# Two layers of a hybrid Fourier, Hyena and attention backbone: two pairs instead of three for the input projection's weights, staging slots for the last first modulation weights, one modulation group in the output projection

## The chip, the cores and the metric

The kernel runs on one core of one Trainium2 chip. The metric is the device time of one execution in microseconds (us); the median of three runs before the change is 2942.47, from 2940.16 to 2943.14. The engines are TensorE (PE in the profile, its weight loads PEld), VectorE (DVE), ScalarE (ACT), GpSimd (POOL) and SyncE (SP); DMAs are issued here by SyncE, GpSimd and ScalarE, each in the order of its own queue.

## What is computed

Two layers on 1024 latent tokens and 256 context tokens of width 1024. Layer 0 mixes with a Fourier transform on half of the channels and a Hyena operator (two long convolutions with generated filters) on the other half, with one input and one output projection; layer 1 is neighbourhood attention. Each layer ends in a modulated feed-forward. The reference, cut:

```python
def ada_mod(cond, w, b):                 # six groups: shift, scale, gate, twice
    m = (jax.nn.silu(cond) @ w + b)[..., None, :]
    return jnp.split(m, 6, axis=-1)

def hyena_filters(L, w1, b1, freq, w2, b2, w3):
    ...
    h = jnp.sin(freq * (z @ w1 + b1))
    h = jnp.sin(freq * (h @ w2 + b2))
    h = (h @ w3).reshape(L, 2, HY_ORDER, HY_CH)
    ...
    h = h / jnp.sum(jnp.abs(h), axis=(0, 1), keepdims=True)
    ...
def mixer_ab(u, w_in, w_out, conv_w, conv_b, w1, b1, freq, w2, b2, w3, skip):
    p = u @ w_in
    y_f = fourier_mix(p[..., :FOURIER_CH])
    y_h = hyena_mix(p[..., FOURIER_CH:], conv_w, conv_b, w1, b1, freq, w2, b2, w3, skip)
    return jnp.concatenate([y_f, y_h], axis=-1) @ w_out
...
    sh1, sc1, g1, sh2, sc2, g2 = ada_mod(c, ada_w[i], ada_b[i])
    u_lat = modulate(rms_norm(h_lat, norm1_g[i]), sh1, sc1)
    ...
    h_lat = h_lat + g1 * y_lat
    h_lat = h_lat + g2 * swiglu(modulate(rms_norm(h_lat, norm2_g[i]), sh2, sc2),
                                ffn_w_gate[i], ffn_w_up[i], ffn_w_down[i])
```

## The kernel before

**Products in pieces.** Activations and weights are split into a high and a low part (`split`, L345 to L352: ScalarE casts the high part at L349, VectorE subtracts for the low part at L351), and a product is three products of parts on TensorE (`mm`, L345). A weight block is loaded into a staging slot of tag `ws` (four slots of 128x1024), and its high and low parts go to `wh` and `wl` (two slots each).

**Pools.** `S4` gives one of 21 tiles of 128x1024, `S2` one of 35 of 128x512; results wait in eight PSUM banks (`ps`, `pq`).

**The order.** The code is a set of generators that are advanced in turn by hand. The instructions are then ordered for each engine by a scheduler that simulates a timeline from its own costs; so the order on an engine follows the code only in part, and tiles' slots are handed out in it. On an engine, and on each DMA queue, instructions run in that order. `ld` puts a load on SyncE's queue (L330), `ldr` on GpSimd's (L336).

**The start.** `ada_first` computes the modulation groups 1 and 0 (scale and shift of layer 0) on TensorE: sixteen tiles of `in_ada_k` (0.5 MB each, GpSimd's queue), each multiplied with the two condition columns into two banks; then `columns` turns the rows into columns (a copy to `g` at L509, eight 2x2 products). Beside it run the filter network (casts and subtractions for its last layer at L734 to L737) and the first norm (squares at L665 on ScalarE and L668 on VectorE).

**The input projection** (`in_proj`) has 16 blocks of 128 output channels. The first two run together, the rest one by one, each with 72 products of 256 or 512 columns. Its weights come by `weights3`, in which every third block's two parts take `ws` slots. Work of other generators is dealt between the eight steps of a block (`filled`) by tables of rates, one number for each block: `long` (the long filters: `filter_raw`, which multiplies the network's output with `in_w3` and a window, `filter_sum` and `spectrum_l`), `filt` (the filters for the context), and `ada`, the modulation groups 2 and 3, whose weights load into `ws` slots and which VectorE reduces (`ada_group`, L567, four instructions a step, eight steps a group).

**From there to the feed-forward.** After the projection the filters' spectra and the transforms of the data follow, then `inverse_last` (the last inverse transforms; L1211 and L1218 add and subtract spectra there, L1376 are its products and L1408 its copies). Group 4 of the modulation runs in the loop over `inverse_last`, with `ws` slots on SyncE's queue. `out_proj` (products L1716) fetches a weight block ahead and takes what is left of that generator. The feed-forward and layer 1 follow; in the second feed-forward the weights' parts alternate between `ws` and `wh`/`wl` slots by the counter `p3`, which `weights3` also advances.

Of the kernel before, what the change touches and what calls it, by code (L numbers as in the profile page):

```python
# [18 lines left out]
P = 128  # L19
# [239 lines left out]
class Builder:  # L259
# [119 lines left out]
    def weights3(self, src):  # L379

        self.p3 = (self.p3 + 1) % 3
        st = self.W("ws", "ws")
        tags = ("ws", "ws") if self.p3 == 0 else ("wh", "wl")
        hi, lo = self.pair2(tags)
        self.ld(st, src)
        self.split(st, hi, lo)
        return hi, lo

# [108 lines left out]
    def ada_first(self):  # L497
# [7 lines left out]
        def columns(m, ps):  # L505
            col = self.PS()
            for j in (0, 1):
                row = self.G()
                nc.vector.tensor_copy(row[0:2, :], ps[j][0:2, :])  # L509
                for k in range(4):  # L510
                    nb = 4 * j + k
                    self.mm(col[:, 2 * nb:2 * nb + 2], row[0:2, k * P:(k + 1) * P], self.ident[0:2, 0:2], True, True)
# [9 lines left out]
        for m in (1, 0):  # L522
            ps[m] = [self.PP(), self.PP()]
            for kb in range(KB):
                w = self.S4()
                self.ldr(w, a["ada_k"][m, kb])
                for j in (0, 1):
                    self.mm(ps[m][j][0:2, :], cond[:, 2 * kb:2 * kb + 2], w[:, j * 512:(j + 1) * 512], kb == 0, kb == KB - 1)
                yield
        columns(1, ps[1])  # L530
        columns(0, ps[0])
# [11 lines left out]
    def ada_group(self, l, m, conds, where):  # L543
# [12 lines left out]
        ready = [load(m * 8)] if where == "ws" else []  # L556
        for nb in range(m * 8, m * 8 + 8):
            if where != "ws" or nb < m * 8 + 7:
# [18 lines left out]
    def late_groups(self, ms):  # L577

        self.load_cond(wide=False)
        for m in ms:  # L580
            yield from self.ada_group(0, m, (0, 1), "ws")
# [166 lines left out]
    def filter_raw(self, sq, raws, os=(0, 1)):  # L748
# [4 lines left out]
        for o in os:  # L753
            for j in (0, 1):
                st[(o, j)] = self.S2()
                self.ld(st[(o, j)], a["w3"][:, (2 * j + o) * HC:(2 * j + o + 1) * HC])
        yield
        for o in os:
            for eo, op in ((0, ADD), (1, SUB)):
# [4 lines left out]
                w3[(o, eo)] = (hi, lo)  # L764
        yield
        for b in range(nb):
            for s, lh in ((0, self.ta[sq]), (1, self.tb[sq])):
                w = self.S2()
                self.ld(w, a["win_" + sq][b, s])
# [261 lines left out]
    def in_proj(self, u, norm, fill, four, conv):  # L1031
# [40 lines left out]
        pairs = [self.weights3(a["w_in"][nb]) for nb in (0, 1)]  # L1072
# [17 lines left out]
        for i, nb in enumerate(order[2:], 2):  # L1090
            wh, wl = self.weights3(a["w_in"][nb])
# [1368 lines left out]
    def run(self):  # L2460
# [28 lines left out]
        def filters():  # L2489
            for o in (0, 1):  # L2490
                tot = self.filter_sum("l", o, raws["l"][o])
                for k, _ in enumerate(self.filter_raw("l", raws["l"], (o,))):
                    if k > 2 and k % 2:
                        next(tot)
                    yield
                yield from self.spectrum_l(o, raws["l"][o], tot)

        long = filters()
        ada = self.late_groups((2, 3))
# [17 lines left out]
        self.in_proj(u, ng, ((long, (4,) * 8 + (6, 0)), (filt, (0,) * 9 + (3, 3, 3, 3, 2)), (ada, (0, 0, 0) + (1,) * 10 + (2,))), fc, cc)  # L2517
# [292 lines left out]
```

## Time and profile before

| | |
|---|---|
| median of three runs | 2942.47 us |
| profiled execution | 2941.1 us, its span 2939.3 |
| granted TensorE clock, mean | 0.974 |
| TensorE, 0 to 68 us (start) | 45.7 us busy |
| TensorE, 68 to 500 us (input projection, filters) | 392 us busy of 432 |
| TensorE, 500 to 590 us (transforms) | 89.0 us busy of 90 |
| TensorE, 590 to 725 us (inverse transforms) | 108.5 us busy of 135 |
| TensorE, 725 to 820 us (output projection) | 95.0 us busy of 95 |
| TensorE, 820 to 2939 us (feed-forward, layer 1) | 2074.7 us busy of 2119 |

The times of the profile count from the span's start. "Busy" includes time at half clock, where a product takes twice as long; the granted clock of a stretch says how much of that there was. In a row of the timeline stand start, duration, engine, line, operation, tiles and the count of instructions run together; in brackets stands the engine's idle time before it and what ended that.

### The profile page before, as it was taken

Reading aid. Unit: us, or ns where it says so; the run is one execution under the profiler, and the core shown is the slowest. Engines: PE = TensorE matmul, PEld = TensorE weight load, DVE = VectorE, ACT = ScalarE, POOL = GpSimd, SP = SyncE. Lnnn points to the kernel's source line nnn. Section 1 sums busy time; section 2 is a strip of 40 time slices with the busy share of each in tenths; the row PEclk is TensorE's granted clock in tenths of the full one; section 3 lists DMA queues with packets and bytes.
Section 4 is the critical chain, followed back from the end, with each engine's and each line's share of the span. In section 5 each row is a group of like instructions: output and inputs, shape, how many; then the busy total and the mean of one; then the engine's idle time right before and its main releaser. Section 6 shows DMA issues by size and latency. Waiting matters only on the chain. (4 is left out here: it accounts for less than half of the span.)

```text
span 2939.3 us, 43728 instructions
## 1 busy us (share of the span) xinstructions
PE 2804.8 (95%) x15570; PEld 2343.3 (80%) x15570; DVE 2078.2 (71%) x3657; ACT 1319.4 (45%) x2259; POOL 538.3 (18%) x867
## 2 busy tenths in 40 slices
PE   6989998978999999999999999999999999999998
PEld 2768776867899888888888988888887788888886
DVE  4677788767586888877777526777777987664555
ACT  2533324533355333333445426777765533333433
POOL 1120232350101121213020002333221022111000
PEclk8999898988999999999999999999999999999999
DMA  6244636674456565658895435678766276434763
GB/s 248 73 164 163 190 94 204 202 232 168 151 193 220 193 202 193 206 195 312 300 311 184 158 115 152 181 184 191 206 213 219 83 266 228 162 110 166 228 194 130
DMA packets 298217, 557.35 MB, mean 190 GB/s; under 512 B 82057, under 2 KB 128331, under 8 KB 297999
## 3 DMA queue, kind: packets, MB, share of 16 engines
q1 hardware_dynamic: 236046, 371.53, 40.8%
q0 software_dynamic: 59648, 178.83, 17.3%
q10 hardware_dynamic: 2304, 4.20, 0.4%
q8 instruction: 123, 2.02, 0.3%
q14 instruction: 96, 0.78, 0.1%
HBM read 407.10 MB, written 119.80 MB: 179 GB/s over the span
## 5 line engine op out<-in xcount | busy, mean ns | idle before, releaser
L1883 PE MATMUL ps<-s,s 128*128 128x512 f32 x1976 | 488.2, 389 | 2.5 <-DVE s L351 1.9
L1883 PEld LDWEIGHTS ps<-s,s 128*128 128x128 f32 x1976 | 370.6, 188 | 80.9 <-DVE s L351 2.6
L345 PE MATMUL ps<-s,wh 128*128 128x256 f32 (+1 forms) x1752 | 404.1, 333 | 8.3 <-DVE s L1026 5.1
L345 PEld LDWEIGHTS ps<-s,wh 128*128 128x128 f32 x1752 | 295.6, 192 | 42.1 <-ACT s L1024 5.3
L345 PE MATMUL pq<-s,wh 128*128 128x512 f32 (+1 forms) x872 | 267.2, 382 | 9.6 <-ACT wh L349 5.5
L345 PE MATMUL ps<-s,wl 128*128 128x256 f32 (+1 forms) x876 | 266.5, 330 | 1.6 <-DVE wl L351 1.5
L349 ACT CAST s<-s 128x1024 fp32r<-128x1024 f32 (+2 forms) x192 | 172.7, 927 | 201.6 <-DMA s<-d 166.2
L2056 PE MATMUL ps<-s,s 128*128 128x512 f32 (+1 forms) x1000 | 259.6, 383 | 3.1 <-DVE s L351 3.0
L351 DVE TENSOR_TENSOR wl<-ws,wh 128x1024 fp32r<-128x1024 f32 (+1 forms) x141 | 167.7, 1190 | 132.9 <-ACT wh L349 128.4
L345 PE MATMUL ps<-s,s 128*128 128x65 f16 (+5 forms) x2754 | 237.9, 239 | 20.1 <-DVE s L351 5.0
L349 ACT CAST wh<-ws 128x1024 fp32r<-128x1024 f32 (+1 forms) x141 | 144.6, 1025 | 231.5 <-PE ps L345 88.2
L349 ACT CAST s<-t 128x512 fp32r<-128x512 f32 (+2 forms) x238 | 133.9, 582 | 240.5 <-PE ps L1883 72.8
L351 DVE TENSOR_TENSOR s<-s,s 128x1024 fp32r<-128x1024 f32 (+2 forms) x170 | 190.8, 1154 | 53.2 <-ACT s L349 50.6
L2056 PEld LDWEIGHTS ps<-s,s 128*128 128x128 f32 x1000 | 184.5, 188 | 41.1 <-DVE s L351 4.8
L351 DVE TENSOR_TENSOR s<-t,s 128x512 fp32r<-128x512 f32 (+2 forms) x238 | 150.8, 649 | 77.5 <-ACT s L349 55.5
L1883 PE MATMUL ps<-s,wh 128*128 128x512 f32 x616 | 191.2, 390 | 0.0
L345 PEld LDWEIGHTS pq<-s,wh 128*128 128x128 f32 x872 | 159.1, 190 | 38.4 <-ACT wh L349 5.9
L345 PEld LDWEIGHTS ps<-s,wl 128*128 128x128 f32 x876 | 164.5, 191 | 18.4 <-DVE wl L351 2.2
L345 PE MATMUL pq<-s,wl 128*128 128x512 f32 (+1 forms) x436 | 166.0, 381 | 0.0
L345 PEld LDWEIGHTS ps<-s,s 128*128 128x128 f32 x834 | 131.2, 199 | 33.6 <-issue 7.7
L2056 PE MATMUL ps<-s 128*128 128x512 f32 (+1 forms) x500 | 150.8, 385 | 0.0
L336 POOL DMA_DIRECT2D d<-s x154 | 83.8, 545 | 359.1 <-DVE s L1690 123.0
(483 smaller groups left out, 5582.5 us busy)
## 6 DMA issues: line engine op xcount, KB each, us to landing
s<-d SPq DMA_DIRECT2D x283, 256.0 KB, 3.9
s<-in_down SPq DMA_DIRECT2D x150, 256.0 KB, 3.9
d<-s POOLq DMA_DIRECT2D x138, 256.0 KB, 3.4
s<-in_ada_w POOLq DMA_DIRECT2D x56, 512.0 KB, 4.9
d<-tk POOLq DMA_DIRECT2D x98, 256.0 KB, 4.3
ws<-in_up SPq DMA_DIRECT2D x44, 512.0 KB, 3.7
d<-g POOLq DMA_DIRECT2D x86, 256.0 KB, 3.0
ws<-in_gate SPq DMA_DIRECT2D x42, 512.0 KB, 3.6
```

The source lines that it names most:

```text
L336: self.last_ldr = self.nc.gpsimd.dma_start(out, in_).ins
L345: self.nc.tensor.matmul(o, l, r, start=st, stop=sp)
L349: self.last_hi = nc.scalar.copy(hi, src).ins
L351: self.last_lo = eng.tensor_tensor(lo, src, hi.bitcast(F32), SUB).ins
L1883: nc.tensor.matmul(ps, x[:, sl], y, start=first and j == 0 and x is wh and y is xh, stop=j == 3 and x is wl, skip_group_check=True)
L2056: m = nc.tensor.matmul(acc[j][:, c0:c1], x[:, sl], y[:, xs], start=first and k == 0, stop=last and k == 2, skip_group_check=True)
```

## The change

1. `weights3` goes. All blocks of the input projection use `weights`: two pairs, `wh`/`wl` alone.
2. In `ada_first` the last two tiles of group 0 load into `ws` slots instead of `S4` tiles, and the columns of both groups are ordered behind the last of the products.
3. Modulation weights are loaded one step ahead in layer 0's groups 0 to 4, whichever slots they use. Groups 2 and 3 stay in the input projection. Group 4 leaves the loop over `inverse_last` and runs in `out_proj` alone, with `S4` tiles on GpSimd's queue.
4. `filter_raw` loads its windows a step ahead; the first filter's `in_w3` loads come before its sum, the second filter's during the spectrum of the first.
5. The rates by which the long filters and the modulation are dealt into the blocks are changed.

```diff
--- before.py
+++ after.py
@@ -376,16 +376,6 @@
         self.split(st[:, :w], hi[:, :w], lo[:, :w])
         return hi, lo
 
-    def weights3(self, src):
-
-        self.p3 = (self.p3 + 1) % 3
-        st = self.W("ws", "ws")
-        tags = ("ws", "ws") if self.p3 == 0 else ("wh", "wl")
-        hi, lo = self.pair2(tags)
-        self.ld(st, src)
-        self.split(st, hi, lo)
-        return hi, lo
-
     def mat(self, w, dt=F32R):
         self.mk ^= 1
         return self.W(("wh", "wl")[self.mk], "mat", dt, w)
@@ -509,7 +499,8 @@
                 nc.vector.tensor_copy(row[0:2, :], ps[j][0:2, :])
                 for k in range(4):
                     nb = 4 * j + k
-                    self.mm(col[:, 2 * nb:2 * nb + 2], row[0:2, k * P:(k + 1) * P], self.ident[0:2, 0:2], True, True)
+                    with self.follow(last):
+                        self.mm(col[:, 2 * nb:2 * nb + 2], row[0:2, k * P:(k + 1) * P], self.ident[0:2, 0:2], True, True)
             sl = slice(m * 8, m * 8 + 8)
             for c in (0, 1):
                 t = self.ada[(0, c)]
@@ -522,13 +513,14 @@
         for m in (1, 0):
             ps[m] = [self.PP(), self.PP()]
             for kb in range(KB):
-                w = self.S4()
+                w = self.W("ws", "ws") if m == 0 and kb > KB - 3 else self.S4()
                 self.ldr(w, a["ada_k"][m, kb])
                 for j in (0, 1):
-                    self.mm(ps[m][j][0:2, :], cond[:, 2 * kb:2 * kb + 2], w[:, j * 512:(j + 1) * 512], kb == 0, kb == KB - 1)
+                    last = nc.tensor.matmul(ps[m][j][0:2, :], cond[:, 2 * kb:2 * kb + 2], w[:, j * 512:(j + 1) * 512],
+                                            start=kb == 0, stop=kb == KB - 1).ins
                 yield
-        columns(1, ps[1])
-        columns(0, ps[0])
+        for m in (1, 0):
+            columns(m, ps[m])
 
     def load_cond(self, conds=(0, 1), wide=True):
         self.cond = []
@@ -553,9 +545,10 @@
             (self.ld if where == "mat" else self.ldr)(t, a["ada_w"][l, nb])
             return [t[:, :512], t[:, 512:]]
 
-        ready = [load(m * 8)] if where == "ws" else []
+        ahead = l == 0 and m < 5
+        ready = [load(m * 8)] if ahead else []
         for nb in range(m * 8, m * 8 + 8):
-            if where != "ws" or nb < m * 8 + 7:
+            if not ahead or nb < m * 8 + 7:
                 ready.append(load(nb + len(ready)))
             st = ready.pop(0)
             for c in reversed(conds):
@@ -574,11 +567,11 @@
                 g = (0 if m == 1 else 2) + l
                 nc.vector.scalar_tensor_tensor(t[:, sl], t[:, sl], 1.0, self.gs[:, g * 8:g * 8 + 8], op0=ADD, op1=MUL)
 
-    def late_groups(self, ms):
-
-        self.load_cond(wide=False)
+    def late_groups(self, ms, where):
+
+        self.load_cond(wide=where == "s4")
         for m in ms:
-            yield from self.ada_group(0, m, (0, 1), "ws")
+            yield from self.ada_group(0, m, (0, 1), where)
 
     def ada_col(self, l, pc, m, b):
         return self.ada[(l, 1 if pc == 2 else 0)][:, m * 8 + b:m * 8 + b + 1]
@@ -754,6 +747,13 @@
             for j in (0, 1):
                 st[(o, j)] = self.S2()
                 self.ld(st[(o, j)], a["w3"][:, (2 * j + o) * HC:(2 * j + o + 1) * HC])
+        ws, todo = [], [(b, s) for b in range(nb) for s in (0, 1)]
+
+        def load():
+            if todo:
+                ws.append(self.S2())
+                self.ld(ws[-1], a["win_" + sq][todo.pop(0)])
+
         yield
         for o in os:
             for eo, op in ((0, ADD), (1, SUB)):
@@ -762,11 +762,12 @@
                 hi, lo = (self.S2(F32R), self.S2(F32R)) if sq == "l" else (self.G(F32R), self.G(F32R))
                 self.split(t, hi, lo)
                 w3[(o, eo)] = (hi, lo)
+        load()
         yield
         for b in range(nb):
             for s, lh in ((0, self.ta[sq]), (1, self.tb[sq])):
-                w = self.S2()
-                self.ld(w, a["win_" + sq][b, s])
+                w = ws.pop(0)
+                load()
                 for o in os:
                     for eo in (0, 1):
                         ps = self.PS()
@@ -1069,7 +1070,7 @@
                 self.ld(self.pd[nb], t)
             return t
 
-        pairs = [self.weights3(a["w_in"][nb]) for nb in (0, 1)]
+        pairs = [self.weights(a["w_in"][nb]) for nb in (0, 1)]
         p01 = [{}, {}]
         for _ in range(4):
             next(norm)
@@ -1088,7 +1089,7 @@
         next(front)
         work = filled(0)
         for i, nb in enumerate(order[2:], 2):
-            wh, wl = self.weights3(a["w_in"][nb])
+            wh, wl = self.weights(a["w_in"][nb])
             acc = {pc: self.PS() for pc in PCS}
             for kb in range(KB):
                 for w, part in ((wh, 0), (wh, 1), (wl, 0)):
@@ -2487,16 +2488,22 @@
         next(ng)
 
         def filters():
+            gens = [self.filter_raw("l", raws["l"], (o,)) for o in (0, 1)]
+            next(gens[0])
+            yield
             for o in (0, 1):
                 tot = self.filter_sum("l", o, raws["l"][o])
-                for k, _ in enumerate(self.filter_raw("l", raws["l"], (o,))):
-                    if k > 2 and k % 2:
+                for k, _ in enumerate(gens[o]):
+                    if k > 1 and k % 2 == 0:
                         next(tot)
                     yield
-                yield from self.spectrum_l(o, raws["l"][o], tot)
+                for k, _ in enumerate(self.spectrum_l(o, raws["l"][o], tot)):
+                    if o == 0 and k == 5:
+                        next(gens[1])
+                    yield
 
         long = filters()
-        ada = self.late_groups((2, 3))
+        ada = self.late_groups((2, 3), "ws")
         filt = (x for o in (0, 1) for g in (self.filter_raw("c", raws["c"], (o,)), self.spectrum_c(o, raws["c"][o]))
                 for x in g)
         self.Y = {}
@@ -2514,13 +2521,14 @@
             yield from self.inverse_c(1, y)
 
         fc, cc = four(), conv()
-        self.in_proj(u, ng, ((long, (4,) * 8 + (6, 0)), (filt, (0,) * 9 + (3, 3, 3, 3, 2)), (ada, (0, 0, 0) + (1,) * 10 + (2,))), fc, cc)
+        self.in_proj(u, ng, ((long, (1, 2, 4, 5, 5, 5, 5, 5, 6, 0)), (filt, (0,) * 9 + (3, 3, 3, 3, 2)),
+                             (ada, (0,) * 5 + (1, 1, 2, 1, 2, 1, 2, 1, 2, 1, 2))), fc, cc)
         self.held = False
         for i in range(8):
             self.tap(f"u{i}", u.ap(0, i, 0))
         drain(long)
         drain(ada)
-        late = self.late_groups((4,))
+        late = self.late_groups((4,), "s4")
         for g in (filt, fc):
             for _ in g:
                 pass
@@ -2552,7 +2560,6 @@
         self.parts()
         for i, _ in enumerate(self.inverse_last(y, self.fourier_l(y))):
             next(cc, None)
-            next(late, None)
         drain(cc)
         for b in range(8):
             self.tap(f"yl{b}", y.ap(0, b, 0))
```

The orders of three places follow, before and after. In them `s`, `t`, `g`, `c` are tiles of working memory, `ps` and `pq` banks, `d` scratch in device memory.

ScalarE at the start, before: the squares of the norm (L665), the first weights' high part (`wh_333`), and the filter network's casts, whose source is the slot `s_42`.

```order
L665 ACTIVATE t_291,c_284<-s_31_122 128x1024
L665 ACTIVATE t_295,c_284<-s_33_126 128x1024
L349 CAST wh_333<-ws_332 128x1024
L734 CAST s_46_166<-s_42_151 64x512
L736 CAST s_47_167<-s_42_151 64x512
L734 CAST s_48_172<-s_42_151 64x128
L736 CAST s_49_173<-s_42_151 64x128
L665 ACTIVATE t_299,c_284<-s_35_130 128x1024
```

The same place after:

```order
L658 ACTIVATE t_291,c_284<-s_31_122 128x1024
L658 ACTIVATE t_295,c_284<-s_33_126 128x1024
L727 CAST s_46_166<-s_42_151 64x512
L729 CAST s_47_167<-s_42_151 64x512
L727 CAST s_48_172<-s_42_151 64x128
L729 CAST s_49_173<-s_42_151 64x128
L658 ACTIVATE t_299,c_284<-s_35_130 128x1024
L658 ACTIVATE t_303,c_284<-s_37_134 128x1024
L349 CAST wh_333<-ws_332 128x1024
```

The four casts now stand ahead of the weights' cast and two of the squares behind them are ahead of it too.

TensorE in the input projection at the start of the fourth block, before (`ps_1112<-s_207` is a Fourier product, `wh_1125` and `wl_1126` are the block's weight):

```order
L345 MATMUL ps_1112<-s_207_728,s_266_876 128x256
L345 MATMUL ps_1112<-s_207_728,s_267_877 128x256
L345 MATMUL ps_1112<-s_207_728,s_266_876 128x256
L345 MATMUL ps_1130<-s_127_344,wh_1125 128x256
L345 MATMUL ps_1130<-s_128_345,wh_1125 128x256
L345 MATMUL ps_1130<-s_127_344,wl_1126 128x256
L345 MATMUL ps_1130<-s_127_344,wh_1125 128x256
L345 MATMUL ps_1130<-s_128_345,wh_1125 128x256
L345 MATMUL ps_1130<-s_127_344,wl_1126 128x256
```

Inside the fourth block after (its weight is `wh_1036` and `wl_1037`, and `s_261` to `s_265` with `s_46_166` or `s_47_167` are filter products):

```order
L345 MATMUL ps_1041<-s_129_346,wl_1037 128x256
L345 MATMUL ps_1042<-s_159_479,wl_1037 128x512
L345 MATMUL ps_1043<-s_187_615,wl_1037 128x512
L345 MATMUL ps_1064<-s_261_927,s_47_167 128x512
L345 MATMUL ps_1064<-s_262_928,s_47_167 128x512
L345 MATMUL ps_1068<-s_264_933,s_47_167 128x512
L345 MATMUL ps_1068<-s_265_934,s_47_167 128x512
L345 MATMUL ps_1103<-s_261_927,s_46_166 128x512
L345 MATMUL ps_1103<-s_262_928,s_46_166 128x512
```

Before, other products stand in front of the block, and its own follow one another undivided; now filter products stand between those of the block.

SyncE's queue from the inverse transforms to the output projection, before (`in_vko_l`: matrices of the last inverse transform; `in_x_t`, `in_ctx_t`: the residual):

```order
L330 DMA ws_5963<-in_ada_w 128x1024
L330 DMA ws_6053<-in_ada_w 128x1024
L330 DMA ws_6135<-in_ada_w 128x1024
L330 DMA ws_6189<-in_ada_w 128x1024
L330 DMA s_1558_6039<-d_329 128x256
L330 DMA cs_6199<-in_vko_l 128x2048
L330 DMA s_1574_6107<-d_330 128x256
L330 DMA cs_6205<-in_vko_l 128x2048
L330 DMA s_1604_6211<-d_328 128x1024
L330 DMA s_1577_6121<-d_331 128x256
L330 DMA s_1605_6213<-d_329 128x1024
L330 DMA s_1606_6215<-d_330 128x1024
```

and, some rows on, the first loads of the output weights:

```order
L330 DMA s_1671_6412<-in_ctx_t 128x512 x2
L330 DMA s_1672_6415<-in_x_t 128x512 x2
L330 DMA s_1673_6418<-in_x_t 128x512 x2
L330 DMA ws_6429<-in_w_out 128x2x512
L330 DMA ws_6435<-in_w_out 128x2x512
L330 DMA ws_6441<-in_w_out 128x2x512
L330 DMA s_1674_6421<-in_x_t 128x512 x2
```

After:

```order
L330 DMA tk_5782<-d_4034 128x512
L330 DMA cs_5863<-in_vi_c 128x512
L330 DMA cs_5867<-in_vi_c 128x512
L330 DMA cs_6115<-in_vko_l 128x2048
L330 DMA cs_6121<-in_vko_l 128x2048
L330 DMA ws_6357<-in_w_out 128x2x512
L330 DMA ws_6373<-in_w_out 128x2x512
L330 DMA ws_6389<-in_w_out 128x2x512
L330 DMA ws_6456<-in_w_out 128x2x512
L330 DMA s_1533_5985<-d_329 128x256
L330 DMA s_1544_6043<-d_330 128x256
L330 DMA s_1547_6057<-d_331 128x256
```

Four modulation loads are gone from between, and the matrices and four loads of output weights now stand ahead of the loads of `d_329` and of the residual.

## The prediction

> **What bounds the kernel now.** First the page's busy shares, then TensorE's busy tenths and its granted clock in 40 slices of 73.5 us.
>
> ```profile
> PE 2804.8 (95%) x15570; PEld 2343.3 (80%) x15570; DVE 2078.2 (71%) x3657; ACT 1319.4 (45%) x2259; POOL 538.3 (18%) x867
> PE   6989998978999999999999999999999999999998
> PEclk8999898988999999999999999999999999999999
> ```
>
> TensorE is busy for 95% of the span and the change removes none of its products, so the change can only win TensorE's idle time and the stretches at a lowered clock. Both lie at the front: the slices with 6 to 8 tenths are 1, 3, 7, 9, 10 and the last. The table of windows cuts the span by stage (columns: length, then busy of PE, PEld, DVE, ACT, POOL, granted clock, DMA share, GB/s).
>
> ```profile
> 0.00:68.00 68.00, 45.69 (x116) 13.95 (x117) 29.58 (x53) 20.23 (x29) 13.82 (x32) 0.87 0.73 268
> 68.00:118.00 50.00, 50.00 (x284) 43.42 (x283) 30.33 (x53) 23.82 (x43) 3.12 (x2) 0.98 0.17 49
> 118.00:250.00 132.00, 113.49 (x539) 90.79 (x538) 91.80 (x187) 50.13 (x99) 25.07 (x42) 0.91 0.50 165
> 250.00:500.00 250.00, 228.45 (x1069) 183.82 (x1068) 201.32 (x444) 86.67 (x165) 46.77 (x63) 0.90 0.49 154
> 590.00:725.00 135.00, 108.48 (x594) 93.29 (x595) 101.42 (x196) 48.35 (x76) 44.05 (x44) 0.86 0.62 209
> 725.00:820.00 95.00, 95.00 (x496) 80.95 (x495) 52.06 (x84) 36.98 (x61) 11.96 (x22) 1.00 0.49 173
> 820.00:2939.00 2119.00, 2074.66 (x12060) 1763.50 (x12058) 1499.29 (x2544) 1003.53 (x1724) 354.71 (x629) 0.99 0.61 196
> ```
>
> The input projection with the filters is 68 to 500: 50.0 + 113.5 + 228.5 = 392 us busy of 432, so 40 us idle. The clock here is full or half, so a mean of 0.91 over 132 us means 24 us at half speed and 0.90 over 250 us means 50; half of that, up to 37 us, is lost too. The inverse transforms (590 to 725) lose 26.5 us idle and up to 19 by the clock. The output projection (725 to 820) loses nothing. The table of 820 to 2939 has little left, and the change touches it least. So the stake is the start, some 70 us in the input projection, and some 40 in the inverse transforms.
>
> **The change part by part.** *The start.* The timeline before:
>
> ```profile
> 23.69 0.19 ACT L665 ACTIVATION_READ_ACCUMULATOR t<-s 128x1 f32 x1
> 30.38 0.08 DVE L668 DVE_READ_ACCUMULATOR2_ANT c<- 128x1 f32 x1
> 35.84 1.04 ACT L349 CAST wh<-ws 128x1024 fp32r<-128x1024 f32 x1 [11.97 <-DMA ws<-in_w_in]
> 36.79 0.61 ACT L734 CAST s<-s 64x512 fp32r<-64x512 f32 x1
> 38.18 0.69 DVE L735 TENSOR_TENSOR s<-s,s 64x512 fp32r<-64x512 f32 x1
> 39.93 0.29 DVE L737 TENSOR_TENSOR s<-s,s 64x128 fp32r<-64x128 f32 x1
> 40.51 2.61 POOL L336 DMA_DIRECT2D s<-in_ada_k  x5 [19.41 <-DVE s L737]
> 31.04 5.31 PE L345 MATMUL ps<-s,c 128*2 128x512 f32 x12 [0.58 <-DMA s<-in_ada_k]
> 44.36 3.57 PE L345 MATMUL ps<-s,c 128*2 128x512 f32 x4 [8.02 <-DMA s<-in_ada_k]
> 64.05 1.05 PE L345 MATMUL pq<-c,g 2*128 2x2 f32 x8
> 68.03 0.78 PE L345 MATMUL ps<-s,wh 128*128 128x256 f32 x2
> DMA  0999999999999999995019999980000000000000
> GB/s 3 175 311 354 397 422 418 422 422 418 420 420 422 420 422 405 399 413 215 0 29 305 371 420 410 420 274 1 0 8 0 0 0 0 4 0 0 0 0 4
> ```
>
> Read as one chain: ScalarE stands 12 us on the weights' DMA with the filter network's casts (L734, L736) queued behind; so VectorE's L737 ends at 40.2, its slot comes free, and only then does GpSimd's queue, 19.41 us late, send the last six modulation tiles. The DMA engines (2-us slices, 0 to 80) are full until 37 us, empty until 41, and full again to 53. TensorE idles 8.02 us and then takes 3.57 us a tile where it took 5.31 / 3 = 1.77. In the new order those casts stand ahead of the weights' cast, behind squares that ended at 23.9, and VectorE's part can follow its last square (30.4) in its two 0.69 and two 0.29 us: the slot is free at 33 to 35, before the queue runs dry. Two of the six tiles no longer need the slot at all. Summing the slices, 12.5 MB had moved by 34 us; the other 5.7 of the 18.24 MB in this view need 5.7 / 0.42 = 14 us, so with no hole everything has landed at about 48. The early pair (1.05 MB) pushes the tiles behind it on GpSimd's queue by 2.5 us, which costs TensorE nothing lasting, since the sum of bytes is unchanged. Four late tiles at 1.77 us give an end of the products at about 51, where the last columns began at 64.05: gain 13. The least is the idle gap alone, 8; the most is an end at 48, 16. The columns, all behind the last tile now, take their 2 x 2 us after it as before (64.05 to 68.03). The first projection product then comes at about 55.
>
> One rule bears on how far these gaps reach. The Trainium skill, "TensorE: Matmul & The Clock Gate", section "What's actually happening", says that the clock halves after an idle window of about 3.4 us and needs about as long a busy one to come back. The trace agrees at the start (8.02 us idle, then 3.57 instead of 1.77 us a tile). By it, gaps under 3.4 us cost only themselves, and the next term would be about 17 instead of 20, the sum -39.
>
> *Input projection, pairs and order.* Stretches between and in blocks:
>
> ```profile
> 117.70:140.60 22.90, 16.71 (x84) 13.95 (x84) 16.35 (x35) 12.18 (x25) 3.29 (x6) 0.85 0.36 127
> 155.40:170.20 14.80, 12.38 (x64) 8.74 (x63) 11.49 (x25) 6.08 (x13) 1.08 (x2) 0.88 0.12 34
> 190.10:209.50 19.40, 12.18 (x60) 8.10 (x59) 10.76 (x19) 7.07 (x11) 2.12 (x4) 0.93 0.63 201
> 209.50:239.10 29.60, 26.93 (x106) 21.43 (x107) 19.54 (x42) 8.48 (x18) 6.47 (x12) 0.82 0.66 214
> L349 ACT CAST wh<-ws 128x1024 fp32r<-128x1024 f32 x13 | 13.6, 1049 | 31.4 <-DMA ws<-in_w_in 18.7 <-DVE c L567 7.1 <-PE ps L345 5.6
> L351 DVE TENSOR_TENSOR wl<-ws,wh 128x1024 fp32r<-128x1024 f32 x13 | 15.8, 1214 | 12.6 <-ACT wh L349 12.6
> 448.32 0.35 SPq L330 DMA_DIRECT2D ws<-in_w_in  x1
> PE pq L345 <- ACT wh L349: 5.5, 1, 5.5
> ```
>
> The first three are stretches between weight blocks, in which TensorE has only filter and Fourier products and waits on their splits: 6.2 + 2.4 + 7.2 us idle. The fourth, a block of weights, adds 2.7. By the clock column (0.15 x 22.9 and so on; twice that at half speed, half of it lost) up to 3.4 + 1.8 + 1.4 + 5.3 = 12 more go, of which I count 10, as some of it falls in idle time: 28 lost. In the new order the filter products are dealt into the weight blocks, whose products are ready and cover the splits, and modulation starts two blocks later, so it no longer holds staging slots here. I take 17 of the 28 (three fifths: the splits themselves stay in VectorE's queue), and 3 of the 5.5-us gap at which a weight load was issued only at 448: gain 20. Least: 5, that one gap, if the filters only wait elsewhere. Most: 28 + 5.5, 34.
>
> What is added: with two pairs, the first cast of block 2 waits for the joint end of blocks 0 and 1, when both pairs come free. Queued behind it on ScalarE are the filters' first splits, for which VectorE's low parts and TensorE's filter products wait. Cast and low part are 1.05 + 1.21 us, partly covered by filter products: loss 1, from 0.5 to 2.5. From block 3 on one pair is always one block (29 us on average in 118 to 500) ahead.
>
> *Modulation group 4.* It leaves the inverse transforms:
>
> ```profile
> 590.43 1.28 SPq L330 DMA_DIRECT2D ws<-in_ada_w  x2
> 597.33 0.74 DVE L567 CUSTOM_DVE_ANT_0 t<-ws,s,c 128x512 f32<-128x512 f32 x1
> 603.01 1.23 DVE L1211 TENSOR_TENSOR s<-ps,s 128x1024 f32<-128x1024 f32 x1 [2.67 <-DMA s<-d]
> 604.29 5.43 PE L345 MATMUL ps<-s,mat 128*128 128x512 f32 x12 [5.38 <-DVE s L1211]
> 657.71 11.99 SPq L330 DMA_DIRECT2D ws<-in_ada_w  x4
> 699.94 5.92 PE L1376 MATMUL ps<-mat,s 128*128 128x256 f32 x48 [2.28 <-ACT tk L1408]
> 703.43 1.62 SPq L330 DMA_DIRECT2D ws<-in_w_out  x3
> 710.34 4.63 PE L1716 MATMUL ps<-s,wh 128*128 128x256 f32 x12 [4.48 <-ACT wh L349]
> L567 DVE CUSTOM_DVE_ANT_0 t<-ws,s,ah 128x512 f32<-128x512 f32 x8 | 6.9, 856 | 0.1
> ```
>
> The reductions are 8 x 4 = 32 at 0.74 to 0.86 us, about 25 us of VectorE. The 5.38-us gap is not ended by them but by a DMA behind two modulation loads on SyncE's queue: 1.05 MB less ahead of it is worth about 2.7, its wait. The four loads at 657.71 held SyncE's queue for 12 us while VectorE worked them off, and the loads of the output weights came at 703.43; in the new order those stand ahead, so the 4.48 and 2.28 go. With some 2.5 us of the 19 lost to the clock the gain is 12. Least: 5, the 4.48 gap and little more. Most: 18, all three gaps (12.1) and a third of the clock's loss.
>
> In the output projection the same 25 us meet 95 - 52 = 43 us of idle VectorE, and eight loads go by GpSimd's queue, idle for 83 of 95; TensorE is hidden as long as its banks are read in time. Were VectorE's cover gone, all 25 would show. Loss 2, from 0 (it fits) to 4 (a few evictions each behind a group of four reductions, 3 us). The other edits move window loads a step earlier on SyncE's queue; they cost nothing as DMA is at half there. The swapped turn of staging slots in the second feed-forward weights (the counter now enters it elsewhere) is 0, +-3.
>
> *Sum* on the profiled execution's 2941.1 us (span 2939.3 and 1.8 around it): -13 + 1 - 20 - 12 + 2 = -42, so 2899. The median of the runs is 1.4 above that execution: 2900.
>
> **The rivals.** (1) *Two pairs are too few, slower.* A cast of the next pair waits for the last product of the block before the last and stands first in ScalarE's queue; if ScalarE or VectorE is more than a block behind, each of the 13 blocks exposes 1.05 + 1.21 us and about 1.7 us of half clock and of the splits behind it: 13 x 4 = 52, less 25 for start and tail, plus the 1 + 2: 2971. It decides once the splits' delay exceeds one block. For it: VectorE has 201 of 250 us taken, and modulation is now denser in just these blocks. Against: only 5.6 us of the casts' waits were on TensorE.
>
> (2) *The input projection gives it back.* VectorE's 80% from 250 on takes the modulation that 118 to 250 is rid of, and new gaps open there: start and tail alone, -13 + 1 - 12 + 2 = -22, 2920. For: modulation is compressed into the last 11 blocks; against: VectorE still has 49 us there.
>
> (3) *The start is bound by bytes.* If early tiles only displace others in full DMA, the start returns just the 4-us hole: -33, 2909. Against: the six tiles were the last needed. The Trainium skill, "DMA: Bandwidth & Descriptors", section "Issuing engines are not separate DMA queues", speaks for it: queues of all engines share 16 DMA engines and interleave. The trace shows that ceiling, about 420 GB/s.
>
> (4) *It does not do what it says*: what stalls is the chain of splits, whatever the order; gains and losses cancel, 2942, within 6.
>
> **How the numbers follow.** Forecast 0.52, (1) 0.13, (2) 0.15, (3) 0.12, (4) 0.08. The terms' ends give -16 + 0.5 - 34 - 18 + 0 = -67.5 and -8 + 2.5 - 5 - 5 + 4 = -11.5, so with the median's 1.4 and the +-3, 2872 to 2934 for the forecast itself. It holds (2) and (3); reaching to 2942 it takes in half of (4) and leaves out (1). About 0.2% (6 us) is what the runs can tell from no change. Faster: forecast, (2), (3) and a little of (4), 0.81; same: most of (4), 0.05; slower: (1) and a rest of (4), 0.14.
>
> **What would show it.** Start: GpSimd's 19.41-us wait shrinks to a few us, TensorE's 8.02-us gap goes, first projection product at 52 to 60; at 64 rival (3) holds. Projection: idle plus clock loss of the stage to the turn (68 to 500) falls from 77 to about 57, the gaps between blocks 2 to 5 shortened; if the casts wait on TensorE for tens of us, (1). Tail: no modulation load on SyncE in the inverse transforms, the output weights issued before the last inverse products, the 4.48 gap gone; output projection still full. I am wrong if the gaps of the projection return after 250, or if the start is held by another transfer.

## The result, and the profile after

The changed kernel takes 2902.11 us (median of three, 2900.75 to 2906.06), before it was 2942.47. The ratio is 0.9868, with a 95% interval from 0.9845 to 0.989: some 39 us faster, where 2900 was forecast. The profiled execution is the longest of the three, 2906.06 us with a span of 2904.3, so stage by stage there are 35 us to find, and not 40.

The page after: TensorE's busy time fell from 2804.8 to 2787.7 us although the count of its products is the same; the mean granted clock rose from 0.974 to 0.983, so this is time at half clock that went.

```profile
PE 2787.7 (96%) x15570; PEld 2332.2 (80%) x15570; DVE 2077.1 (72%) x3657; ACT 1320.5 (45%) x2259; POOL 542.4 (19%) x875
PE   7999898989999999999999999999999999999998
PEclk9999899989999999999999999999999999999999
```

The windows after, cut where TensorE has done about as much of its work as at the cuts before (columns as there: length, busy of PE, PEld, DVE, ACT, POOL, clock, DMA share, GB/s):

```profile
0.00:57.50 57.50, 41.31 (x116) 12.74 (x116) 28.02 (x51) 19.49 (x28) 13.77 (x32) 0.99 0.89 326
57.50:110.40 52.90, 52.44 (x304) 45.58 (x303) 37.10 (x70) 27.43 (x52) 6.77 (x8) 0.98 0.19 61
110.40:222.50 112.10, 107.64 (x531) 85.78 (x530) 78.45 (x151) 43.39 (x84) 21.64 (x37) 0.95 0.48 154
222.50:473.70 251.20, 222.63 (x1063) 179.33 (x1062) 211.88 (x465) 91.90 (x171) 49.50 (x63) 0.93 0.52 166
564.70:679.10 114.40, 102.17 (x600) 90.17 (x599) 75.68 (x123) 45.48 (x70) 47.06 (x52) 0.91 0.65 224
679.10:776.60 97.50, 95.64 (x493) 80.68 (x492) 77.19 (x156) 41.70 (x69) 11.88 (x22) 1.00 0.53 194
776.60:2904.30 2127.70, 2076.95 (x12053) 1764.70 (x12052) 1496.78 (x2542) 1003.12 (x1723) 353.49 (x629) 0.99 0.61 195
```

The start is 10.5 us shorter. In the projection the part from 110 to 222 takes 112 us instead of 132 and idles 4.5 where it idled 18.5; the part behind it idles 29 us where it idled 21.5, and is no shorter. The inverse transforms are some 20 us shorter, the output projection 2.5 longer, and the last window 9 longer than the one before.

The start's timeline after (start, duration, engine, line, operation, tiles, count, idle before):

```profile
24.93 0.60 ACT L727 CAST s<-s 64x512 fp32r<-64x512 f32 x1
34.64 1.56 POOL L336 DMA_DIRECT2D s<-in_ada_k  x3 [10.69 <-DVE s L730]
41.38 7.03 PE L519 MATMUL ps<-s,c 128*2 128x512 f32 x16 [1.21 <-DMA s<-in_ada_k]
48.24 3.60 PE L519 MATMUL ps<-ws,c 128*2 128x512 f32 x8
51.77 1.94 PE L345 MATMUL ps<-c,g 2*128 2x2 f32 x16
57.52 0.78 PE L345 MATMUL ps<-s,wh 128*128 128x256 f32 x2
```

The casts stand at 24.93 instead of 36.79, the slot comes free at 34.6, the 8.02-us gap is 1.21, and the products end at 51.8. GpSimd still waits 10.69 us for the slot, not the few us that were expected, but TensorE has tiles to work on meanwhile. The first projection product starts at 57.5.

In the tail, a row of TensorE's timeline before that the prediction does not show, then its timeline and SyncE's queue after:

```profile
658.26 1.31 PE L345 MATMUL pq<-mat,s 128*128 128x256 f32 x3 [3.57 <-ACT s L349]
```

```profile
573.75 3.01 PE L345 MATMUL ps<-s,mat 128*128 128x512 f32 x12 [1.81 <-DVE s L1212]
578.84 4.58 PE L345 MATMUL pq<-s,mat 128*128 128x512 f32 x12 [2.08 <-DVE s L1212]
623.80 0.51 PE L345 MATMUL pq<-mat,s 128*128 128x256 f32 x2 [1.24 <-ACT s L349]
```

```profile
617.30 2.76 SPq L330 DMA_DIRECT2D cs<-in_vko_l  x2
622.16 18.49 SPq L330 DMA_DIRECT2D ws<-in_w_out  x4
```

The 5.38-us gap is 1.81, that of 3.57 is 1.24, and the output weights are asked for from 622 on, 42 us before the first product that uses them (664.0); that gap is gone, and so is the 2.28 before it.

### The profile page after: what moved, and what is told of

Read it like the earlier page. It is cut to its first block, busy times and chain, and to the rows that moved or that the text cites. A ratio compares the mean times of both kernels' runs of the same rounds, so it can differ in the third digit from the quotient of the medians.

```text
span 2904.3 us, 43705 instructions
## 1 busy us (share of the span) xinstructions
PE 2787.7 (96%) x15570; PEld 2332.2 (80%) x15570; DVE 2077.1 (72%) x3657; ACT 1320.5 (45%) x2259; POOL 542.4 (19%) x875
## 5 line engine op out<-in xcount | busy, mean ns | idle before, releaser
L1884 PEld LDWEIGHTS ps<-s,s 128*128 128x128 f32 x1976 | 371.7, 188 | 82.1 <-ACT tk L1889 4.0
L345 PE MATMUL ps<-s,wl 128*128 128x256 f32 (+1 forms) x892 | 272.6, 331 | 2.2 <-DVE wl L351 2.1
L345 PE MATMUL pq<-s,wh 128*128 128x512 f32 (+1 forms) x840 | 255.1, 381 | 3.9 <-DVE s L2643 2.9
L345 PE MATMUL ps<-s,s 128*128 128x65 f16 (+4 forms) x2748 | 233.7, 237 | 18.2 <-DVE st L2377 3.8
L2057 PEld LDWEIGHTS ps<-s,s 128*128 128x128 f32 x1000 | 184.4, 188 | 41.6 <-DVE s L351 5.1
L345 PEld LDWEIGHTS pq<-s,wh 128*128 128x128 f32 x840 | 152.9, 190 | 31.6 <-DVE s L2643 3.3
L345 PE MATMUL pq<-s,wl 128*128 128x512 f32 (+1 forms) x420 | 159.4, 379 | 0.0
L345 PEld LDWEIGHTS ps<-s,s 128*128 128x128 f32 (+1 forms) x828 | 128.9, 195 | 27.4 <-ACT t L2379 4.0
```

Of the source, the lines that this page charges most:

```text
L345: self.nc.tensor.matmul(o, l, r, start=st, stop=sp)
L1884: nc.tensor.matmul(ps, x[:, sl], y, start=first and j == 0 and x is wh and y is xh, stop=j == 3 and x is wl, skip_group_check=True)
L2057: m = nc.tensor.matmul(acc[j][:, c0:c1], x[:, sl], y[:, xs], start=first and k == 0, stop=last and k == 2, skip_group_check=True)
```

## The experiments

Twelve kernels ran, in four groups; "before" ran beside each on the same chip. A row of this table has the ratio to before with its interval, and five landmarks of the profiled execution: the first projection product, the first VectorE instruction of the transforms (L1218 in the lines of before, "the turn"), the first and the last product of line L1716, and the span. L1716 is the first part of the output projection, its first four blocks; the rest of the output projection counts here to what follows. The differences of neighbouring landmarks are the stages.

| kernel | ratio | 95% | first product | turn | first, last of L1716 | span |
|---|---|---|---|---|---|---|
| before | 1 | | 68.0 | 501.0 | 710.3, 748.4 | 2939.3 |
| changed | 0.9868 | 0.9845-0.989 | 57.5 | 473.1 | 664.0, 704.8 | 2904.3 |
| d_start | 0.995 | 0.993-0.997 | 58.1 | 488.6 | 695.1, 732.8 | 2924.3 |
| d_group4 | 0.9895 | 0.9873-0.9918 | 65.9 | 492.7 | 677.8, 718.9 | 2913.8 |
| d_pairs | 1.0002 | 0.9988-1.0016 | 66.9 | 498.4 | 706.0, 743.8 | 2939.4 |
| d_feed | 0.998 | 0.9969-0.9992 | 65.9 | 494.1 | 701.7, 738.7 | 2928.7 |
| all_again | 0.9886 | 0.9869-0.9903 | 61.8 | 476.8 | 665.5, 705.7 | 2905.0 |
| d_startgroup | 0.9887 | 0.9871-0.9904 | 58.9 | 487.1 | 671.2, 711.0 | 2905.0 |
| d_feedpairs | 0.9979 | 0.9964-0.9993 | 63.4 | 485.5 | 692.6, 730.9 | 2928.7 |
| u_group4 | 0.9943 | 0.9925-0.9961 | 57.5 | 471.4 | 679.9, 718.2 | 2919.4 |
| d_g4queue | 0.9986 | 0.9973-1.0 | 67.3 | 496.8 | 703.5, 741.5 | 2936.6 |
| u_parity | 0.9879 | 0.9861-0.9897 | 57.1 | 474.1 | 662.3, 703.9 | 2906.1 |
| d_start_ws | 0.9988 | 0.9975-1.0001 | 66.1 | 489.5 | 698.6, 736.4 | 2929.9 |
| d_g4short | 0.9964 | 0.9951-0.9978 | 63.5 | 499.0 | 698.6, 736.4 | 2932.5 |

### One part alone

Each of these is the kernel before with some parts of the diff above: part 2 (start), part 3 (group 4), part 1 (pairs), parts 4 and 5 (filter loads and rates).

d_start:

```diff
-                w = self.S4()
+                w = self.W("ws", "ws") if m == 0 and kb > KB - 3 else self.S4()
...
+                    with self.follow(last):
```

> The kernel before with part 2 alone (last two modulation tiles in staging slots, columns behind the last product). My theory, that the start is a stage of its own: the first projection product moves from 68.0 to about 57.5 us, as in the changed kernel, and the rest of the program keeps its time: 2942 - 10.5 = 2932. Rival, that the scheduler's cast order at the start comes from the other parts: GpSimd's queue still waits some 19 us for its slot, the first product stays at 65 to 68, time 2939 to 2943.

Measured 0.995, the first product at 58.1: the start moves without the other parts, and brings 15 us here (9 to 21), more than the 10 by which the first product moves.

d_group4:

```diff
+        ahead = l == 0 and m < 5
...
-        late = self.late_groups((4,))
+        late = self.late_groups((4,), "s4")
...
-            next(late, None)
```

> The kernel before with part 3 alone (modulation loads a step ahead in layer 0, group 4 in the output projection through GpSimd's queue). My theory: the inverse transforms to the output projection's end shrink by the 19 us that the changed kernel shows there, of which about 4 return in the first feed-forward: 2926 to 2929, and the four modulation loads vanish from SyncE's queue. Rival, that the gain comes from elsewhere (an earlier end of the input projection's DMAs): the gaps of 5.4 and 4.5 us at the inverse transforms' start and end stay, 2938 to 2943.

Measured 0.9895, 31 us (24 to 37) and more than I expected. From the turn to the first output product it takes 185.1 us instead of 209.3, and the L1716 part of the output projection 41.1 instead of 38.1. Another 6 us of the profile lie in the projection stage (426.8 us instead of 433.0), where the order on TensorE is word for word that of before; that is taken up in the last section.

d_pairs:

```diff
-            wh, wl = self.weights3(a["w_in"][nb])
+            wh, wl = self.weights(a["w_in"][nb])
```

> The kernel before with part 1 alone (two pairs for the projection's weights, old rates). My theory: a cost only, 1 to 5 us, 2943 to 2947, since the gaps in the filters' splits stay. Rival, that the freed staging slots are what shortens the input projection: the gaps of 5.1 us at 209 and 5.5 at 454 go, 2925 to 2932.

Measured 1.0002: no change. The slots that the third pair frees bring nothing alone, and two pairs cost nothing that these runs can tell. The gaps of 5.1 us at 209 and 5.5 at 454 are gone from its profile, as the rival had it, but others stand in their place (3.55 at 158, 4.67 at 285), and the projection stage takes 431.5 us.

d_feed:

```diff
-((long, (4,) * 8 + (6, 0)), ..., (ada, (0, 0, 0) + (1,) * 10 + (2,)))
+((long, (1, 2, 4, 5, 5, 5, 5, 5, 6, 0)), ..., (ada, (0,) * 5 + (1, 1, 2, 1, 2, 1, 2, 1, 2, 1, 2)))
```

> The kernel before with parts 4 and 5 alone (windows loaded a step ahead, new rates), three pairs kept. My theory, that the dealing is what shortens the input projection: 68 to the turn loses 17 us, 2925, mostly by fewer stretches at half clock. Rival, that the new rates need the freed slots: modulation, two steps in a block, waits for staging slots that the third pair holds, and the stage keeps its 432 us or grows: 2940 to 2955.

Measured 0.998, 6 us: between the two. TensorE's timeline shows one long wait, at a weight's low part:

```profile
268.25 1.44 PE L345 MATMUL ps<-s,wl 128*128 128x256 f32 x3 [6.53 <-DVE wl L351]
```

It is not the rival's wait for a slot: ScalarE had cast the high part at 245.7, and VectorE worked without a pause from 249.8 until the low part at 267.0, on filter work and four of the modulation's reductions that stand ahead of it.

### Parts together

all_again is the changed kernel once more, for this group.

> The changed kernel again, as the base for the other three of this group on the same chip: 0.986 to 0.987 of the kernel before, 2900 to 2903 if before is 2940.

d_startgroup has parts 2 and 3 of the diff and nothing of 1, 4 and 5.

> The kernel before with parts 2 and 3 alone (start and group 4); three pairs, old rates and old window loads. My theory, that the parts add and that pairs and dealing together bring some 5 us: 2940 - 11 - 28 = 2901, at most 5 above the changed kernel. Rival, as I had it in the prediction, that the input projection's dealing brings 17 to 20 us of the 40: 2917 to 2922, 15 or more above the changed kernel.

Measured 0.9887 beside 0.9886 for the whole change: 2905.90 and 2905.83 us. Each has an interval of some 5 us either way; within that, parts 2 and 3 are the whole gain. My own picture of the prediction, that the projection's dealing brings half of it, falls as a statement on the time. The parts do not simply add, either: alone, parts 2 and 3 bring 15 and 31 us, together 33 (28 to 38). The 12 or so that are missing are a little more than the intervals allow (about 10).

d_feedpairs has parts 1, 4 and 5, and nothing of 2 and 3.

> The kernel before with parts 1, 4 and 5 (two pairs, windows a step ahead, new rates), the start and group 4 as before. My theory after the parts alone: about 5 us under before, 2935. Rival, that pairs and rates work only together (slots that the third pair frees are used by the denser modulation): 17 to 20 under before, 2920 to 2923, and the gaps of 4 us and more in the input projection go.

Measured 0.9979, 6 us (2 to 11), as the parts alone had it. But its projection stage (63.4 to 485.5) takes 422.1 us, where before took 433.0; so something is won there and lost behind it.

u_group4 is the changed kernel with one part undone:

```diff
             next(cc, None)
+            next(late, None)
...
-        late = self.late_groups((4,), "s4")
+        late = self.late_groups((4,), "ws")
```

> The changed kernel with group 4 put back into the loop over the last inverse transforms, with staging slots on SyncE's queue. My theory: 19 to 28 us come back, 2920 to 2930, with modulation loads on SyncE's queue ahead of the output weights and the gap of 4 to 6 us at the output projection's first product. Rival, that the earlier input projection gives the queue enough lead and only the 25 us of reductions move: 2905 to 2912.

Measured 0.9943 against 0.9886: 17 us back, where group 4 alone had brought 31. The stage from the turn takes 208.5 us again, and its timeline has the old gaps:

```profile
574.20 5.37 PE L345 MATMUL ps<-s,mat 128*128 128x512 f32 x12 [5.23 <-DVE s L1212]
627.63 1.31 PE L345 MATMUL pq<-mat,s 128*128 128x256 f32 x3 [3.51 <-ACT s L349]
679.93 4.63 PE L1717 MATMUL ps<-s,wh 128*128 128x256 f32 x12 [5.26 <-ACT wh L349]
```

### What in group 4 costs, and what in the start gains

d_g4queue (the kernel before, one queue changed):

```diff
-                self.ld(t, a["ada_w"][l, nb])
+                (self.ldr if m == 4 else self.ld)(t, a["ada_w"][l, nb])
```

> The kernel before with one thing changed: group 4's eight weight loads go by GpSimd's queue instead of SyncE's; its staging slots, its 32 reductions and their place in the loop over the last inverse transforms stay. My theory, that the cost of group 4 there is VectorE's 25 us and the staging slots it holds from the output weights: a small gain, 0 to 8 us (0.997 to 1.000 of before), the gaps at the splits (3.6 and 2.1 us at 658 and 665) and at the output projection's first product (4.5) stay. Rival, that it is the four loads waiting at the head of SyncE's queue: 15 to 28 us (0.990 to 0.995), the matrices of the last inverse transform and the output weights then come early.

Measured 0.9986, 4 us, with an interval that reaches 1.0; the stage takes 206.7 us. SyncE's queue is not the main cost. The output weights still come late, and the gap stays:

```profile
703.54 4.51 PE L1716 MATMUL ps<-s,wh 128*128 128x256 f32 x12 [6.09 <-ACT wh L349]
```

d_g4short (the kernel before):

```diff
-                    nc.vector.tensor_tensor_reduce(o, st[j], self.cond[c][j], 1.0, init, MUL, ADD, to)
+                    n = 32 if l == 0 and m == 4 else 512
+                    nc.vector.tensor_tensor_reduce(o[:, :n], st[j][:, :n], self.cond[c][j][:, :n], 1.0, init, MUL, ADD, to)
```

> The kernel before with group 4's 32 reductions cut to the first 32 of 512 columns each (the group's values are then incomplete: part of the second modulation is left out); its loads, staging slots, queue and places in the loop stay. My theory, that VectorE's 25 us between the last inverse transforms' steps are the cost: 15 us or more less, 0.990 to 0.995 of before, the gaps of 3.6 and 2.1 us at the splits (658, 665) gone, the gap of 4.5 at the output weights perhaps left. Rival, that the staging slots and the place of the loads are the cost (the output weights get their slots and their turn on SyncE only when the group is through): 0 to 6 us, 0.998 to 1.000, and the gap of 4.5 us at the output projection's first product stays.

Measured 0.9964, 11 us (6 to 14): less than my 15, more than the rival's 6. The stage takes 199.6 us. Its timeline is against both: the 3.57 at the split stays (3.44), with VectorE rid of the reductions, and the 4.48 before the first output product is gone, with the loads still on SyncE's queue and in their staging slots (the first output weight is asked for at 687.2, before at 703.4).

```profile
601.64 5.49 PE L345 MATMUL ps<-s,mat 128*128 128x512 f32 x12 [4.29 <-DVE s L1212]
655.64 1.31 PE L345 MATMUL pq<-mat,s 128*128 128x256 f32 x3 [3.44 <-ACT s L349]
698.55 0.88 PE L1717 MATMUL ps<-s,wh 128*128 128x256 f32 x4
```

So of the 24 us by which d_group4's stage is shorter than that of before (209.3), the reductions alone are worth 7 to 10. The queue alone is worth 3 at most, and perhaps nothing: kernels that leave group 4 as it was take 206.5 to 209.3 for this stage. The other half comes with neither; whether it needs the slots free, the loads gone or all of it together is not separated here.

d_start_ws (the kernel before):

```diff
-                w = self.S4()
+                w = self.W("ws", "ws") if m == 0 and kb > KB - 3 else self.S4()
```

> The kernel before with half of part 2: the last two modulation tiles in staging slots, but the columns of both groups not ordered behind the last product. My theory, that the slots alone give the early casts and with them the gain: 0.995 of before, first projection product at 57 to 60 us. Rival, that the columns between the products, which let TensorE wait for VectorE's copies, are half of it: 0.9975, first product at 62 to 64.

Measured 0.9988, first product at 66.1: the rival, and more than it. The DMA hole is gone and the tiles have landed, since the DMA engines fall idle at 46; yet TensorE's timeline has this:

```profile
47.46 1.80 PE L345 MATMUL ps<-c,g 2*128 2x2 f32 x8 [4.44 <-DVE g L509]
50.11 7.39 PE L528 MATMUL ps<-s,c 128*2 128x512 f32 x12
57.34 3.60 PE L528 MATMUL ps<-ws,c 128*2 128x512 f32 x8
66.08 0.78 PE L345 MATMUL ps<-s,wh 128*128 128x256 f32 x2
```

```profile
DMA  0899999999999999999999900000002940000002
```

The columns of the first group stand between the products, wait 4.44 us for VectorE's copy, and hold up tiles that are there; the three tiles behind take 7.39 us instead of 5.31, at a granted clock of 0.71. It is the order of the columns that turns early tiles into an early end. That order without the slots was not run.

u_parity (the changed kernel):

```diff
-        self.held = False
+        self.held, self.p3 = False, 1
```

> The changed kernel with the slot counter p3 set back, before the feed-forward, to the value that it had there in the kernel before, so that gate and up weights take their slots in the old turn. My theory, that this counter is why every kernel with two pairs loses 3 to 4 us between 920 and 960 (time of before) in the first feed-forward: the gap of 2.7 us at the weight cast there goes, 3 to 4 us less than the changed kernel, about 0.986 of before. Rival, that the condition loads for group 5 come too late there whatever the slots: no change, 0.987 to 0.989, the gap stays.

Measured 0.9879 beside 0.9886 and 0.9868 for the changed kernel: no change. The gap at the weight cast shrinks to 1.36 us and the time does not; my theory on the counter falls.

## Why the prediction was right, and where its sum was not

The total and its sign came as forecast, and most of the signs that were named for it. One sign against it came too: gaps of the projection returned in its later part. By its terms, with stages from the table:

**Start, -13.** It came to -10.5 in the changed kernel's profile. The chain was read rightly (casts ahead, slot early, hole gone), and the end of the products at 51 was 51.8. The columns behind them then took 5.7 us to the first projection product, and not 4. And I put the columns' reordering at nothing of its own, as "behind the last tile now", and the gain does not come without that step: the first product stands at 66.1 with the slots alone, at 58.1 with both. The rival of the full DMA engines did not hold: the landing was early in d_start_ws, and what then held TensorE was VectorE's copy.

**Input projection, -20 + 1.** The stage went from 433.0 to 415.6 us, -17.4; by means, five kernels with two pairs and new rates (changed, all_again, u_parity, u_group4, d_feedpairs) take 416.7 (413.9 to 422.2), seven with neither (before, d_start, d_start_ws, d_startgroup, d_group4, d_g4queue, d_g4short) 429.6 (423.4 to 435.6): -13. Idle time and clock loss together came down from 77 to 57 us, as the prediction's sign had it. The form was not what I wrote: idle time fell only from 40 to 33 us, since some of the gaps came back after 222, and the rest is clock. In d_feedpairs TensorE idles 43 us, no less than in before, and the stage is still 11 us shorter. In the changed kernel the gaps became smaller (of four over 3 us one is left; all_again has three, u_parity two), and fewer were followed by half speed: 0.91 and 0.90 became 0.95 and 0.93. The one row of TensorE's timeline in that stage with a gap of over 3 us:

```profile
193.11 0.57 PE L345 MATMUL ps<-s,c 128*2 128x512 f32 x1 [3.79 <-ACT s L349]
```

The Trainium skill, "TensorE: Matmul & The Clock Gate", section "What's actually happening", has the clock halve after an idle window of about 3.4 us. In this trace it halves after less: at 380.9, behind 3.4 us in which TensorE was busy for half the time and no gap was over 0.96 us. No gap from 222.5 to 473.7 is over 2.9 us, and the clock there is 0.93; one place, with TensorE's row and the windows before, in and behind the half clock:

```profile
332.17 0.50 PE L345 MATMUL ps<-g,s 128*128 128x512 f32 x1 [2.88 <-ACT g L349]
329.60:333.10 3.50, 0.61 (x2) 0.30 (x2) 3.50 (x8) 1.60 (x3) 2.90 (x2) 1.00 0.69 208
333.10:343.30 10.20, 6.31 (x24) 5.46 (x25) 10.13 (x31) 1.63 (x6) 0.55 (x2) 0.50 0.53 169
343.40:346.80 3.40, 3.40 (x20) 2.95 (x20) 3.21 (x10) 2.09 (x5) 0.46 (x1) 1.00 0.40 145
```

The prediction used that rule only to make the term smaller, by letting gaps under 3.4 us cost themselves alone; they cost more here. What changed is the share of the long ones: half clock beside gaps of over 3 us took 34 us of the stage before (at 128, 207, 453 and 487) and takes 7 after (at 193), and the rest of the half clock, beside shorter gaps or none, is some 43 us in both profiles. So long gaps cut into short ones returned their clock and little of their idle time.

**Where that term failed** is behind its stage: I summed the stages as independent and gave the one difference that I saw behind the output projection "0, +-3". The same five kernels take 2200.0 us from the last L1716 product to the end (2197.8 to 2202.2), the seven others 2193.7 (2191.0 to 2196.1): +6. And with group 4 gone, the stage from the turn takes 189.3 us (three kernels) after the new projection, 184.6 (two) after the old: +5. 13 won, 11 given back, which fits d_startgroup's 2905.90 against 2905.83. With group 4 in its old place that stage gives nothing back (208.5 in u_group4, 207.1 in d_feedpairs); there the projection's parts keep 6 us in d_feedpairs, and 2, within the intervals, in u_group4 beside d_start. One place where time is lost behind the stage is in the second feed-forward, in the changed kernel's TensorE; before and d_startgroup have no such gap, and it is there with 2.5 and 2.4 us in all_again and u_parity:

```profile
2659.87 2.42 PE L1884 MATMUL ps<-s,s 128*128 128x512 f32 x7 [3.39 <-ACT tk L1889]
```

The scheduler orders the whole program from its own timeline, so an edit at 100 us can move rows at 2660. What all of the 11 us is made of stays open, as does what parts 2 and 3 lose beside each other.

**Group 4, -12 + 2.** The changed kernel's stage is 18.4 us shorter and the L1716 part 2.7 longer: -16; between d_start and d_startgroup the stage goes from 206.5 to 184.1 and the L1716 part from 37.7 to 39.8: -20. The loss of 2 was sized rightly; the gain, put at 12, came to 18 to 22, since I gave the clock 2.5 of its 19 us (TensorE's busy time there fell by 6.3) and left the split's gaps at 658 and 665 standing. The step that laid the gaps to loads on SyncE's queue did not hold: with group 4's loads on GpSimd's queue (d_g4queue) the 5.38 is still 4.46 and the 4.48 is 6.09; it is with the reductions cut (d_g4short) that the latter goes.

By stages the changed kernel's profile has -10.5 - 17.4 - 18.4 + 2.7 + 8.6 = -35, where the terms gave -42. Group 4's larger gain and the give-back behind it offset each other; that the total fits so well is in part luck.

Rival (1), casts that wait for a pair: the mechanism exists and costs nothing. In the projection the casts' waits on TensorE are 15.7 us, against 5.6 before, while TensorE's matmuls wait 0.5 us in all for weights' parts, and d_pairs took 1.0002:

```profile
L349 ACT CAST wh<-ws 128x1024 fp32r<-128x1024 f32 x14 | 14.7, 1049 | 27.3 <-PE ps L345 15.7 <-DMA ws<-in_w_in 11.6
```

Rival (2), that only start and tail count, was the better description of where the time comes from, though its price of 2920 was not: start and group 4 are worth 33 us and not 22, and what the projection gained was returned mostly later rather than inside it.

No kernel tried is clearly faster than the changed one; d_startgroup equals it, within the intervals, with parts 2 and 3 alone.

## What to carry to other kernels

A stage's gain in one profile is not yet a gain in time: build the kernel with the other parts alone, and look at what the stages behind it do, above all where a scheduler orders the whole program. To bring a late operand early, also look at what stands in its consumer's queue ahead of it. On a tail with gaps, count what follows each gap at half clock, and not its idle time alone.

## What was not expected of the hardware

The same stage with the same order of products varies by its clock. Before, d_group4, d_g4queue and d_g4short have the same products in the same order on TensorE up to the turn, and their projection stages take 433.0, 426.8, 429.5 and 435.5 us. The windows of before and d_group4 over exactly this stage show where the difference is:

```profile
68.03:501.00 432.97, 392.92 (x1892) 318.84 (x1891) 324.42 (x683) 161.00 (x305) 75.95 (x107) 0.91 0.46 145
65.93:492.73 426.80, 386.34 (x1892) 313.17 (x1891) 323.96 (x683) 160.99 (x305) 75.98 (x107) 0.93 0.46 147
```

The 1892 products are the same, and TensorE idles 40 us in both (40 to 41 in all four); what differs is the time that the products take, at a higher or lower clock. How much half speed follows gaps of nearly the same size is not the same in every execution. A difference of up to 9 us in one profile of this stage is within that, and needs means over kernels or timed rounds.
